# 100 instead of 96 tokens through gathered expert rows, with other transfers, another softmax placing and four gather buffers

## Chip, core and metric

One core of a Trainium2 chip. The metric is device time in microseconds (us) from launch to end; the median of three runs is given. Engines are named as in the profile: PE (matrix engine), DVE (vector), ACT (scalar), POOL (general), SP (queue that issues most loads). Everything is float32 unless noted.

## What is computed

One decoder layer for 256 tokens of width 2048. After attention and a first layer norm, x goes through a retrieval layer ("PEER"), and then through a gated embedding and a third norm. The retrieval layer is what the change is about:

```python
q = (xt @ wq).reshape(t, PEER_HEADS, PEER_QDIM)
...
va, ia = lax.top_k(sa, PEER_TOPK)
vb, ib = lax.top_k(sb, PEER_TOPK)
cand = (va[..., :, None] + vb[..., None, :]).reshape(t, PEER_HEADS, PEER_TOPK * PEER_TOPK)
cidx = (ia[..., :, None] * PEER_NKEYS + ib[..., None, :]).reshape(t, PEER_HEADS, PEER_TOPK * PEER_TOPK)
top, sel = lax.top_k(cand, PEER_TOPK)
eidx = jnp.take_along_axis(cidx, sel, axis=-1)
gates = jax.nn.softmax(top, axis=-1)
...
    act = jax.nn.gelu(jnp.einsum('thed,td->the', u[eb], xb).astype(jnp.float32))
    return jnp.einsum('the,thed->td', (gb * act).astype(xb.dtype), v[eb])
```

With 8 heads and 16 choices a head, each token uses 128 of 16384 rows of u and of v, each row 2048 numbers (8 KB).

## The kernel before

**Two ways for the experts.** `GROUPS` (L42) names the tokens whose expert rows are fetched one by one: tokens 0 to 63 and 64 to 95, `NSP` = 96 in all. The other `NDT` = 160 tokens are done densely: all 16384 experts are multiplied on PE, and the gates of those not chosen are zero.

*Dense path.* `u_block` (L903) loads 128 experts (1 MB, through SP, five buffers `WF` in turn), multiplies them with the 160 tokens (16 matmuls of 128x128 by 160 columns, which the profile shows as 32 instructions at L206), and ACT writes their gelu to the tile A (L906). `gate_work` (L838) makes the gate matrix from one-hot products on PE (L867, L868; five tokens in a group, L882), and DVE multiplies A by it (L877). `v_block` (L967) then multiplies A with v, 512 KB and 16 matmul instructions (L956) in each of 256 blocks. Two v blocks share a load.

*Gathered path.* `sparse_work` (L770) is a generator whose steps are put between the blocks. A step issues a mark (a tiny load on SP, L812), a copy on POOL that waits for the mark (L813, it paces), and an indirect DMA on POOL (L815) that fetches 128 rows, 1 MB, into one of `NGB` = 3 buffers `gb`. For a group of n tokens 128/n partitions hold each token, so n gathers serve the group, once for u and once for v: 96 + 96. `use` (L792) consumes a gather `NGB` - 1 steps later: for u a product and sum with the token's own row in `xq` (L794), for v a scaled addition to `y` (L798, L800). `sparse_out` (L825) adds the partitions of a token with matmuls against a 0/1 matrix `sel` (L832) and ACT copies the result to `yT` (L835).

*Order of work.* `gathers(n)` (L762) adds n to an account and runs one step for each whole unit: `GQ` = 1.3 for each of the last 13 of 16 query products (L206 into `ps_q`), `GU` = 0.715 for each u block, `GV` = 0.3575 for each v block. The rest is run off after block 108 of the second half of the v blocks (L1030), and `sparse_out` comes after block 113 (L1033). The last `STAG` = 6 v blocks are held back and run bank by bank (L1042), with `res2` (L1005: transposes on PE, residual and statistics on DVE) between them; the first half of `res2` is done at L1035 inside the loop.

*Top-k and gates.* `topk_work` (L730) is another generator. For the first 128 tokens each head's chain (DVE, with a product on POOL, L684) ends in `head_slots` (L715), which computes the expert numbers (L718) and places them by DMA (`place`, L722) in the index tile `eig` from which the gathers read. Then comes `gates(0)` (L697): subtract the maximum on DVE (L700), Exp on ACT (L702), sum, reciprocal and product on DVE; then the chain for tokens 128 to 255 (`topk_heads(1, ...)`), one step for each u block.

The order inside an engine's queue is made by a planner before the launch; it may move an instruction ahead of others, but those wrapped in `keep` stay in program order among themselves. An engine works its queue strictly in order, PE's weight loads aside. ACT's gelu at L906 is not kept, the Exp at L702 is.

## Time and profile before

| | us |
|---|---|
| median of three runs | 1829.22 |
| lowest, highest | 1827.53, 1829.93 |
| the profiled execution | 1826.57 |
| its span, first to last instruction | 1824.6 |
| PE busy in the span | 1786.7 |

The span starts at the first instruction; positions below are microseconds from there. The retrieval layer lies between 415 and 1708: queries 415 to 534, u blocks 534 to 1116, v blocks 1119 to 1703. The gate products run from 858 to 1265. A row of the view by stretches gives, for each engine, its busy time and in brackets its instructions, then the clock granted to PE (1.00 is full), the busy share of the 16 DMA engines, and GB/s. A row of the view by groups reads: line, engine, operation, output<-inputs, shape, count | busy us, mean ns of one | idle time before them and what ended it.

### The profile page before, as it was taken

Reading aid. Unit: us, or ns where it says so; the run is one execution under the profiler, and the core shown is the slowest. Engines: PE = TensorE matmul, PEld = TensorE weight load, DVE = VectorE, ACT = ScalarE, POOL = GpSimd, SP = SyncE. Lnnn points to the kernel's source line nnn. Section 1 sums busy time; section 2 is a strip of 40 time slices with the busy share of each in tenths; the row PEclk is TensorE's granted clock in tenths of the full one; section 3 lists DMA queues with packets and bytes.
Section 4 is the critical chain, followed back from the end, with each engine's and each line's share of the span. In section 5 each row is a group of like instructions: output and inputs, shape, how many; then the busy total and the mean of one; then the engine's idle time right before and its main releaser. Section 6 shows DMA issues by size and latency. Waiting matters only on the chain.

```text
span 1824.6 us, 30303 instructions
## 1 busy us (share of the span) xinstructions
PE 1786.7 (98%) x12094; PEld 1679.9 (92%) x12094; DVE 1045.2 (57%) x1643; ACT 544.4 (30%) x1365; POOL 500.6 (27%) x579
## 2 busy tenths in 40 slices
PE   8999999999999999999999999999999999999896
PEld 6888888888899999999999999999999999999766
DVE  5555588654677894543554544975433333343686
ACT  5677477642010001002333331862000000001532
POOL 0133033006445242322222212222234233220241
PEclk9999999999999999999999999999999999999998
DMA  7554644668789999999999999999999999996561
GB/s 278 187 171 163 231 145 156 231 212 266 306 316 374 420 420 416 395 420 401 415 379 383 380 391 353 420 419 350 421 421 420 415 416 415 419 421 267 212 258 53
DMA packets 98717, 599.33 MB, mean 328 GB/s; under 512 B 13072, under 2 KB 14912, under 8 KB 35600
## 3 DMA queue, kind: packets, MB, share of 16 engines
q1 hardware_dynamic: 66768, 384.24, 54.4%
q0 software_dynamic: 30080, 208.57, 28.5%
q10 hardware_dynamic: 1728, 4.59, 0.7%
q8 instruction: 95, 1.56, 0.3%
q14 instruction: 46, 0.38, 0.1%
HBM read 590.96 MB, written 6.29 MB: 327 GB/s over the span
## 4 chain that ended last, share of the span: by engine, by line
PE 82%; issue 6%; DVE 5%; DMA 4%; POOL 2%; ACT 1%; SPq 0%; DVEq 0%; POOLq 0%; ACTq 0%
PE ps_v L956 30%; PE ps_u L206 23%; PE ps_qk L195 7%; PE ps_qk L197 3%; PE ps_q L206 2%; PE ps_v L214 2%; PE ps_v L215 2%; PE ps_v L213 2%; PE ps_mix L213 1%; PE ps_mix L214 1%; PE ps_mix L215 1%; DMA wf<-peer_u 1%; PE ps_gate L214 1%; PE ps_gate L213 1%; PE ps_gate L215 1%
## 5 line engine op out<-in xcount | busy, mean ns | idle before, releaser
L206 PE MATMUL ps_u<-XF,wf 128*128 128x160 f32 x4096 | 572.4, 301 | 6.8 <-ACT A L906 6.6
L956 PE MATMUL ps_v<-A,wf 128*128 128x160 f32 x4096 | 569.1, 301 | 0.6 <-DVE A L877 0.6
L206 PEld LDWEIGHTS ps_u<-XF,wf 128*128 128x128 f32 x4096 | 560.3, 191 | 9.7 <-ACT A L906 8.8
L956 PEld LDWEIGHTS ps_v<-A,wf 128*128 128x128 f32 x4096 | 558.5, 191 | 1.6 <-DVE A L877 0.7
L800 DVE SCALAR_TENSOR_TENSOR y<-gb,ew,y 128x2048 f32<-128x2048 f32 x94 | 220.9, 2350 | 242.0 <-DMA gb<-v_rows,eig 241.8
L108 DVE TENSOR_TENSOR wl<-wf,wh 128x1024 fp32r<-128x1024 f32 (+1 forms) x201 | 222.7, 1132 | 98.3 <-ACT wh L107 97.0
L794 DVE SCALAR_TENSOR_TENSOR gb<-gb,xq 128x2048 f32<-128x2048 f32 x96 | 218.7, 2286 | 93.3 <-DMA gb<-u_rows,eig 90.5
L107 ACT CAST wh<-wf 128x1024 fp32r<-128x1024 f32 (+1 forms) x201 | 172.8, 889 | 111.7 <-PE ps_qk L195 29.4
L815 POOL DMA_INDIRECT gb<-u_rows,eig x96 | 101.3, 1055 | 334.4 <-DVE gb L794 213.9
L195 PE MATMUL ps_qk<-X,wh 128*128 128x512 f32 x512 | 185.2, 401 | 0.0
L815 POOL DMA_INDIRECT gb<-v_rows,eig x96 | 115.8, 1206 | 196.8 <-DVE y L800 148.8
L906 ACT ACTIVATE A<-ps_u 128x160 f32<-128x160 f32 x128 | 38.5, 303 | 434.7 <-PE ps_u L206 389.4
L813 POOL COPY pace<-mark 1x1 f32<-1x1 f32 x192 | 95.3, 496 | 252.1 <-DMA mark<-c_iota 251.4
L197 PE MATMUL ps_qk<-X,wl 128*128 128x256 f32 x512 | 146.1, 285 | 0.0
L859 ACT ACTIVATE hi<-eq,ghf 128x64 f16<-128x64 f16 x320 | 107.3, 335 | 52.5 <-DVE eq L853 48.5
L195 PEld LDWEIGHTS ps_qk<-X,wh 128*128 128x128 f32 x512 | 96.6, 189 | 21.9 <-issue 1.0
L206 PE MATMUL ps_q<-XF,wf 128*128 128x256 f32 x512 | 113.5, 380 | 0.0
L853 DVE TENSOR_TENSOR eq<-io,iaT 128x320 f16<-128x320 f16 x64 | 31.2, 488 | 133.8 <-ACT lo L860 133.8
L206 PEld LDWEIGHTS ps_q<-XF,wf 128*128 128x128 f32 x512 | 96.2, 191 | 12.0
L860 ACT ACTIVATE lo<-eq,glf 128x64 f16<-128x64 f16 x320 | 107.0, 334 | 0.0
L197 PEld LDWEIGHTS ps_qk<-X,wl 128*128 128x128 f32 x512 | 96.4, 188 | 2.5 <-issue 1.3
L835 ACT COPY XF<-ps_y 128x512 f32<-128x512 f32 x3 | 1.8, 585 | 253.2 <-PE ps_y L832 253.2
(232 smaller groups left out, 1791.2 us busy)
## 6 DMA issues: line engine op xcount, KB each, us to landing
wf<-peer_u SPq DMA_DIRECT2D x128, 1024.0 KB
wf<-peer_v SPq DMA_DIRECT2D x128, 1024.0 KB
wf<-w_qk SPq DMA_DIRECT2D x64, 512.0 KB
wf<-w_out SPq DMA_DIRECT2D x32, 512.0 KB
wf<-peer_wq SPq DMA_DIRECT2D x16, 1024.0 KB
wf<-ple_gate SPq DMA_DIRECT2D x16, 1024.0 KB
wf<-w_v SPq DMA_DIRECT2D x31, 512.0 KB
mark<-c_iota SPq DMA_DIRECT2D x192, 0.0 KB
```

The lines of the kernel that those rows point to most:

```text
L107: self.order(nc.scalar.copy(wh, src))
L108: self.order(nc.vector.tensor_tensor(wl, src, wh.bitcast(F32), op=ALU.subtract))
L195: nc.tensor.matmul(ps, wh[:, j * P:(j + 1) * P], xt[:, dt, :], start=dt == 0, stop=False)
L197: nc.tensor.matmul(ps[:, :T], wl[:, j * P:(j + 1) * P], xt[:, dt, :T], start=False, stop=dt == ND - 1)
L206: nc.tensor.matmul(ps[:, :T - t0], wf[:, dt * P:(dt + 1) * P], xt[:, dt, t0:], start=dt == 0, stop=dt == ND - 1)
L794: keep(nc.vector.scalar_tensor_tensor(g, g, 1.0, xq[i], op0=ALU.mult, op1=ALU.mult, accum_out=eact[i][:, j:j + 1]))
L800: keep(nc.vector.scalar_tensor_tensor(ys[i], g, ew[i][:, j:j + 1], ys[i], op0=ALU.mult, op1=ALU.add))
L813: keep(nc.gpsimd.tensor_copy(pace, mark))
L815: keep(nc.gpsimd.indirect_dma_start(out=g, out_offset=None, in_=a[kind], in_offset=bass.IndirectOffsetOnAxis(ap=eig[i][:, 0, j:j + 1], axi ...
L859: nc.scalar.mul(hi[:, j, :], eq[:, j, :], ghf[:, t])
L860: nc.scalar.mul(lo[:, j, :], eq[:, j, :], glf[:, t])
L956: return nc.tensor.matmul(ps[:, (j % 2) * NDT:(j % 2 + 1) * NDT], vf[:, j * P:(j + 1) * P], W_of(ia), start=False, stop=ia == NIA - 1 and ...
```

## The change

1. A third group of 4 tokens: 100 gathered tokens, 200 gathers, 156 dense tokens. Its rows share buffers with the first group (`tag=f"xq{i % 2}"`), are loaded when the second group's gather number 8 is issued, and its sum `y` lies in the gather buffer itself.
2. Four gather buffers; paces 1.8, 0.7 and 0.35.
3. A token's 128/n partitions are neighbours (before: n apart). So the expert numbers, the gates and the rows of a group each go by one DMA; for the rows the source is read 128/n times by a broadcast. A DVE copy into the new tile `es` orders the numbers of a whole group first. `sel` follows.
4. `gates(0)` runs beside the top-k of the other tokens: the subtraction after its fourth step, the Exp two steps later, the sum six steps after that. The gathered path multiplies no gate in before `gated` is set.
5. The rest of the gathers is run off after v block 119 (before: 108), `sparse_out` comes after block 121 (before: 113), and all of `res2` lies between the held blocks, whose matmuls are now kept in order. The two early loads of gate weights move from after blocks 116 and 119 to after 113 and 117.

```diff
-GROUPS = ((0, 64), (64, 32))
+GROUPS = ((0, 64), (64, 32), (96, 4))
-NGB = 3
-GQ = 1.3
-GU = 0.715
-GV = 0.3575
+NGB = 4
+GQ = 1.8
+GU = 0.7
+GV = 0.35
...
+    es = tkl.tile([P, 2, PH * TOPK], U32, name="es")
...
+        yield
+        yield
         keep(nc.scalar.activation(g, g, AF.Exp))
-        yield
+        for _ in range(6):
+            yield
         keep(nc.vector.tensor_reduce(gs[:, t], g, axis=AX.X, op=ALU.add))
...
-                place(i, slice(0, PH), 1)
+                slots(i, 1, by_slot(i, 1))
+            gated.append(t)
...
+    def slots(i, w, src):
+        t0, n = GROUPS[i]
+        nc.gpsimd.dma_start(eig[i][:, w],
+                            src[t0:t0 + n].rearrange("t (r j) -> t r j", j=n))
+    def by_slot(i, w):
+        t0, n = GROUPS[i]
+        src = eg[t0:t0 + n, w].bitcast(F32)
+        if n < PH:
+            return eg[:, w].rearrange("t h k -> t (h k)")
+        dst = es[t0:t0 + n, w].bitcast(F32)
+        nc.vector.tensor_copy(dst.rearrange("t (r h c) -> t h r c", h=PH, r=P // n),
+                              src.rearrange("t h (r c) -> t h r c", r=P // n))
+        return es[:, w]
     def head_slots(h):
...
-        place(0, slice(h, h + 1), 0)
-    def place(i, hs, w):
-        t0, n = GROUPS[i]
+        t0, n = GROUPS[0]
         m = n // PH
-        dst = eig[i].rearrange("p w (h m) -> p w h m", h=PH)
-        for q in range(P // n):
-            nc.gpsimd.dma_start(dst[q * n:(q + 1) * n, w, hs],
-                                eg[t0:t0 + n, w, hs, q * m:(q + 1) * m])
+        nc.gpsimd.dma_start(eig[0][:, 0, h * m:(h + 1) * m],
+                            eg[t0:t0 + n, 0, h].rearrange("t (r c) -> t r c", c=m))
...
-            place(i, slice(0, PH), 0)
-        yield from gates(0)
-        yield from topk_heads(1, 0, PH)
+            slots(i, 0, by_slot(i, 0))
+        second, first = topk_heads(1, 0, PH), gates(0)
+        for step in range(24):
+            next(second)
+            if step > 2:
+                next(first, None)
+            yield
+        yield from second
...
+        def tokens(i):
+            t0, n = GROUPS[i]
+            xq.append(gin.tile([P, D], F32, name=f"xq{i}", tag=f"xq{i % 2}"))
+            nc.gpsimd.dma_start(xq[i], a["s_x1"][t0:t0 + n, None, :].to_broadcast([n, P // n, D]))
+        tokens(0)
+        tokens(1)
...
-            if acts:
+            if acts and gated:
...
-                ys[i] = gin.tile([P, D], F32, name=f"y{i}", tag=f"xq{i}")
+                if i < 2:
+                    ys[i] = gin.tile([P, D], F32, name=f"y{i}", tag=f"xq{i}")
+                else:
+                    ys[i] = g
...
+                    if kind == "u_rows" and (i, j) == (1, 2 * NGB):
+                        tokens(2)
...
-        if ia == NIA - STAG - 14:
+        if ia in (NIA - STAG - 9, NIA - STAG - 5):
+            sg2.order = keep
+            parts0 += list(sg2.parts(a["ple_gate"][0, len(parts0) // 4]))
+        if ia == NIA - STAG - 3:
             while not run(sparse, 1):
                 pass
-        if ia == NIA - STAG - 9:
-            sparse_out()
-        if ia in (NIA - STAG - 8, NIA - STAG - 7):
-            for t in range(NT):
-                res2(t, 4 * (ia - NIA + STAG + 8), 4)
-        if ia in (NIA - STAG - 6, NIA - STAG - 3):
-            sg2.order = keep
-            parts0 += list(sg2.parts(a["ple_gate"][0, len(parts0) // 4]))
     held = [v_load(1, ia) for ia in range(NIA - STAG, NIA)]
-    for b in range(4):
-        for ia in range(NIA - STAG, NIA):
-            for j in (2 * b, 2 * b + 1):
-                v_mm(psv2[b], j, ia, held[ia - NIA + STAG])
-        v_out(1, b, psv2[b])
-        if b < 3:
-            for t in range(NT):
-                res2(t, 8 + 2 * b, 2)
+    sparse_out()
+    between = [(), ((0, 4),), (), ((4, 4), (8, 2)), (), ((10, 2),), (), ((12, 2),)]
+    for j in range(8):
+        for d0, nd in between[j]:
+            for t in range(NT):
+                res2(t, d0, nd)
+        for ia in range(NIA - STAG, NIA):
+            keep(v_mm(psv2[j // 2], j, ia, held[ia - NIA + STAG]))
+        if j % 2:
+            v_out(1, j // 2, psv2[j // 2])
```

More of the change, by code (lines that the diff above doesn't have):

```diff
@@ L655, in build @@
     keep = tc.keep_in_program_order
+    gated = []
     def topk_heads(t, h0, n):
@@ L719, in head_slots @@
                                        ibN[:NSP, 0, c], op0=ALU.mult, op1=ALU.add)
-        place(0, slice(h, h + 1), 0)
-    def place(i, hs, w):
-        t0, n = GROUPS[i]
+        t0, n = GROUPS[0]
         m = n // PH
-        dst = eig[i].rearrange("p w (h m) -> p w h m", h=PH)
-        for q in range(P // n):
-            nc.gpsimd.dma_start(dst[q * n:(q + 1) * n, w, hs],
-                                eg[t0:t0 + n, w, hs, q * m:(q + 1) * m])
+        nc.gpsimd.dma_start(
+            eig[0][:, 0, h * m:(h + 1) * m],
+            eg[t0:t0 + n, 0, h].rearrange("t (r c) -> t r c", c=m))
     def topk_work():
@@ L772, in sparse_work @@
         xq = []
-        for i, (t0, n) in enumerate(GROUPS):
-            xq.append(gin.tile([P, D], F32, name=f"xq{i}", tag=f"xq{i}"))
-            for q in range(P // n):
-                nc.gpsimd.dma_start(xq[i][q * n:(q + 1) * n, :], a["s_x1"][t0:t0 + n, :])
+        def tokens(i):
[4 more added lines that the diff above has]
+        tokens(1)
         made = []
@@ L1191, in _constants @@
         "c_ident": np.eye(P, dtype=np.float32),
-        **{f"c_sel{i}": (np.arange(P)[:, None] % n == np.arange(n)[None, :]).astype(np.float32)
+        **{f"c_sel{i}": (np.arange(P)[:, None] // (P // n) == np.arange(n)[None, :]).astype(np.float32)
            for i, (_, n) in enumerate(GROUPS)},
```

6 lines of the change are left out of this document (3 added, 3 removed).

## The prediction

> **What bounds the kernel now.** I read the page's first part and its groups first, then the view by stretches, then the DMA view of two stretches.
>
> ```profile
> PE 1786.7 (98%) x12094; PEld 1679.9 (92%) x12094; DVE 1045.2 (57%) x1643; ACT 544.4 (30%) x1365; POOL 500.6 (27%) x579
> ...
> L206 PE MATMUL ps_u<-XF,wf 128*128 128x160 f32 x4096 | 572.4, 301 | 6.8 <-ACT A L906 6.6
> L956 PE MATMUL ps_v<-A,wf 128*128 128x160 f32 x4096 | 569.1, 301 | 0.6 <-DVE A L877 0.6
> ```
>
> PE is busy for 98% of the span, and two groups of 4096 dense matmuls with 160 columns are 1141 us of it. What makes these shorter shortens the kernel, as long as their loads come in time. That second half is read from the stretches.
>
> ```profile
> core 0: us, PE busy (x) PEld busy (x) DVE busy (x) ACT busy (x) POOL busy (x), PEclk, DMA share, GB/s
> ...
> 415.00:534.00 119.00, 119.00 (x590) 105.96 (x589) 74.40 (x243) 15.28 (x39) 63.59 (x73) 1.00 0.80 285
> 534.00:560.00 26.00, 26.00 (x194) 26.00 (x193) 19.85 (x67) 4.01 (x7) 11.45 (x14) 1.00 0.94 367
> 560.00:570.00 10.00, 6.86 (x38) 6.62 (x38) 5.97 (x11) 2.48 (x6) 6.59 (x12) 0.83 0.99 377
> 570.00:635.00 65.00, 65.00 (x481) 65.00 (x480) 53.24 (x163) 4.64 (x16) 19.31 (x32) 1.00 1.01 405
> 635.00:670.00 35.00, 32.67 (x233) 31.40 (x232) 34.00 (x86) 2.52 (x9) 7.17 (x12) 1.00 1.01 420
> 670.00:860.00 190.00, 188.67 (x1391) 187.63 (x1390) 90.96 (x109) 19.34 (x62) 59.82 (x77) 1.00 1.00 411
> 860.00:1116.00 256.00, 256.00 (x2091) 254.06 (x2090) 127.79 (x160) 91.06 (x371) 54.40 (x77) 1.00 0.97 386
> 1116.00:1276.00 160.00, 159.22 (x1375) 155.19 (x1374) 115.52 (x127) 79.09 (x321) 42.41 (x56) 1.00 0.96 389
> 1276.00:1650.00 374.00, 374.00 (x2755) 374.00 (x2755) 144.74 (x62) 1.70 (x4) 110.75 (x119) 1.00 1.01 419
> ```
>
> The last two columns matter. In the query stage the DMA engines move 285 GB/s. From 570 on they are full (share 1.01) at 405 to 420, again from 1276 on at 419. Between, where the gate products slow PE down, 386 to 389 suffice. So two stretches have PE and DMA at their limits together.
>
> ```profile
> DMA packets 18716, 132.56 MB, mean 407 GB/s; under 512 B 2531, under 2 KB 2563, under 8 KB 2563
> ...
> q1 hardware_dynamic: 10467, 75.50, 56.6%
> q0 software_dynamic: 8224, 56.70, 42.7%
> ```
> ```profile
> DMA packets 21589, 156.53 MB, mean 419 GB/s; under 512 B 2504, under 2 KB 2504, under 8 KB 2504
> ...
> q1 hardware_dynamic: 12334, 89.04, 57.5%
> q0 software_dynamic: 8940, 65.00, 41.9%
> q10 hardware_dynamic: 288, 2.10, 1.4%
> ```
> ```profile
> q1 hardware_dynamic: 1472, 10.62, 51.0%
> q0 software_dynamic: 1421, 10.36, 50.0%
> ```
>
> These are the stretches 534:860, 1276:1650 and 590:640: q1 carries the weights, q0 the gathers, in MB. In 590:640 both queues have work all the time, and each gets half, 10.4 to 10.6 MB in 50 us, some 210 GB/s. A weight load of 1 MB (1.0486 million bytes) then takes 4.98 us. PE needs one each 4.35 us (32 instructions). So **gathers that are late take weights away from PE**:
>
> ```profile
> 561.81 0.31 ACT L702 ACTIVATE gate<-gate 128x128 f32<-128x128 f32 x1 [16.81 <-DVE gate L700]
> ```
> ```profile
> 563.79 6.42 PE L206 MATMUL ps_u<-XF,wf 128*128 128x160 f32 x33 [3.14 <-ACT A L906]
> ```
> ```profile
> 640.04 4.58 PE L206 MATMUL ps_u<-XF,wf 128*128 128x160 f32 x32 [0.41 <-ACT A L906]
> 645.01 4.59 PE L206 MATMUL ps_u<-XF,wf 128*128 128x160 f32 x32 [0.39 <-ACT A L906]
> 649.99 4.59 PE L206 MATMUL ps_u<-XF,wf 128*128 128x160 f32 x32 [0.38 <-ACT A L906]
> ```
>
> From 640 blocks start 4.97 us apart, the time of a load at half the bandwidth; I read the named releaser, ACT, as wrong there, since its gelu follows each block at once. The stall at 560 is another thing: ACT sits 16.81 us at the Exp of the first softmax, because DVE is late with the subtraction, the gelus behind it wait, and PE runs out of banks for 3.14 us. The clock of 0.83 in 560:570 costs 1.7 us more.
>
> **The change part by part.**
>
> *Fewer columns.* Rows of the chain of waits give the price of a column:
>
> ```profile
> 443.73 6.91 PE ps_q L206 x32
> ...
> 1275.97 386.85 PE ps_v L956 x2848
> ...
> 1662.83 7.07 PE ps_y L832 x64
> ```
>
> 256 columns: 6.91/32 = 215.9 ns; 160 columns: 386.85/2848 = 135.8 ns. That is 0.834 ns a column. With 64 or 32 columns an instruction still takes 7.07/64 = 110.5 ns, a floor well below 156 columns (132.5). Four columns less are 3.34 ns, for 8192 instructions 27.3 us: by share of the instructions 7.7 in 534:860, 9.4 in 860:1276, 9.2 in 1276:1650 and 1.0 after. The gate products fall from 640 to 624, each of 194 ns but overlapped:
>
> ```profile
> L868 PE MATMUL ps_G<-lo,ohb 128*128 128x64 f16 x320 | 33.5, 194 | 0.1
> ```
>
> Sixteen less save between 0 and 3.1 us; 0.5 taken, since the stretch shows them 10 at a time inside PE's busy time.
>
> *The third group in sparse_out.* 16 matmuls, 32 instructions of 4 columns, at the floor: 32 x 110.5 ns = +3.5 us, all on PE (between 0.4 at 4 columns' price and 3.5).
>
> So **PE alone** would give -27.3 - 0.5 + 3.5 = -24.3 us. The rest is what the loads and waits make of it.
>
> *The u blocks up to 860.* How many gathers are late when they begin:
>
> ```profile
> 415.00:534.00 119.00, 24.91 (x22) 12.25 (x12) 1.00 0.80 285
> 534.00:860.00 326.00, 121.15 (x106) 60.23 (x55) 0.99 1.00 407
> ```
>
> These are the same stretches for the tile gb alone: POOL issued 12 gathers before 534, while the accounts say 16 (13 x 1.3), so 4 to 5 are late. Now 23 are due. What holds them is not bandwidth (285) but the chain head by head: POOL waits for DVE's product, places the numbers, issues as many gathers as buffers are free, and DVE waits for the first of them:
>
> ```profile
> L794 DVE SCALAR_TENSOR_TENSOR gb<-gb,xq 128x2048 f32<-128x2048 f32 x96 | 218.7, 2286 | 93.3 <-DMA gb<-u_rows,eig 90.5
> ```
>
> A fourth buffer lets one more go in each of seven rounds, and one placing DMA of two falls away; each also costs DVE 2.29 us, 16 us for seven, in a queue that is busy 74.4 of 119. Between 0 and 7 more get done; I take 4, 16 by 534, so 7 are late. By block 72 (860) the accounts fall from 51.5 to 50.4 gathers. Before, 54 were moved (56.70/1.0486), 2.5 of the late ones made good. Now 4.6 are to be made good to stand the same, and the row load for the third group adds one: 56, 58.7 MB. With 75.5 of weights and 0.4 of rest 134.6 MB. At 407 GB/s that is 331 us, at 419, the full rate, 321; I take 325. PE alone would need 326 - 7.7 = 318 with today's stalls and 305.5 without (72 blocks of 4.24 us). So **the DMA queue, not PE, ends this stretch: 325 instead of 326, -1 in place of -7.7**. The softmax stall lies inside: while PE waits, gathers catch up. Its Exp comes five blocks (21 us) later in the program; DVE's subtraction comes later as well (16 us of products, then three top-k steps and three gathers at 5 us), so I do not count on the 4.8 us. The bounds: 310 if nothing is made good, 342 if none of the seven gets done.
>
> *860 to 1276.* DMA at 386 to 389 leaves 8% of room, PE ends: -9.4 - 0.5 = -9.9. DVE, busy 243 of 416, has room for the added gathers' 2.3 us each; it would be late next only where it is full (34.0 of 35 in 635:670).
>
> *1276 to 1650.* The same 86 loads (89.04 MB), 60.3 gathers (63.2 MB), 2.1 and 0.4: 154.7 MB, at 419 GB/s 369.3 us; PE wants 364.8. So between -9.2 and -4.7; with a load or so drawn from the five buffers, -7.
>
> *The end.* Less columns -1.0, the third group +3.5. And the wait for the last sum:
>
> ```profile
> 1634.91 0.96 POOL L815 DMA_INDIRECT gb<-v_rows,eig  x1 [0.16 <-issue]
> ```
> ```profile
> 1650.45 2.35 DVE L800 SCALAR_TENSOR_TENSOR y<-gb,ew,y 128x2048 f32<-128x2048 f32 x1 [3.90 <-DMA gb<-v_rows,eig]
> ```
> ```profile
> 1662.66 7.23 PE L832 MATMUL ps_y<-sel,y 128*128 128x64 f32 x64
> ```
>
> DVE ended at 1652.8, PE came at 1662.7: 9.9 us of slack. The last gather was due after block 105, eight blocks before sparse_out; now it is due at 119, two before. Six blocks of 2.12 us are 12.7 us, so PE waits 2.9 us; from 0 to 7 (a fourth gather in flight lands up to 5 us later, or the buffer is free earlier). Taken: +3. Behind it on PE's queue the held matmuls and the transposes of res2, which have no other cover. DVE's and ACT's share of res2 moves between the held blocks at the same work: 0. Sum of the end: +5.5.
>
> *At nothing.* POOL issues some 16 DMAs less; DVE makes three ordering copies and SP issues eight marks more. None of it ends a stretch, since PE and the full DMA queues cover it; where it hurries or holds the head chain, it does so within the bounds of the late gathers.
>
> *A rule against it.* Loading the rows:
>
> ```profile
> xq<-s_x POOLq DMA_DIRECT2D x2, 512.0 KB, 10.0
> xq<-s_x POOLq DMA_DIRECT2D x4, 256.0 KB, 13.4
> ```
>
> Both were read from 64 or 32 rows. The third group's 1 MB has 4 rows as its source's outer dimension. If it ran on 4 of 16 engines, it would take 1.0486 MB/(419/4 GB/s) = 10 us alone and 20 us beside the weights, and the gathers behind it on those engines as long; weights at half rate for 20 us cost PE 20 x (1 - 4.24/4.98) = 3 us. The Trainium skill, DMA: Bandwidth & Descriptors, "Why a DMA increments its semaphore by 16 and not by 1", says that the number of engines is the largest up to 16 that divides the outer dimension of both sides, which would make it 4; it notes exceptions for this queue. No run here shows it. It is a rival below, not in the sum.
>
> **Sum.** -1 - 9.9 - 7 + 5.5 = -12.4 us. The profiled execution, 1826.6 (span 1824.6 and 2.0 around it), would become 1814.2; it stood 2.65 under the median of 1829.22, so the median becomes **1816.8**.
>
> **The rivals.**
>
> - *PE gets all of it* (0.18): the fourth buffer and the idle DMA of the query stage keep gathers in time, and the softmax stall goes: -24.3 - 4.8 = -29.1, 1800. For it: 285 GB/s before 534. Against it: the head chain, not the bandwidth, holds gathers.
> - *The seven stay late* (0.10): 11 late at 534, 9 made good: 139 MB, 332 to 342 us, +11 in place of -1: -0.4, 1829, no change.
> - *Four engines for one load* (0.05): +3, 1820.
> - *Slower: ACT stands at the Exp* (0.12). Price: ACT stood 16.8 us and PE 3.1, so the banks cover 13.7. In the u blocks PE may stall 19.5 us (325 - 305.5) before this ends the stretch rather than DMA. It is slower by more than 3.7 us when PE stalls 36, of which 1.7 is clock, so ACT waits 48: the subtraction at about 607 if ACT comes at 559, after block 6. My estimate is 592 (561.5 + 16 + 15), a stall of some 21 that DMA asks for anyway. With 55 us of waiting: +11, 1840. For it: DVE was 97% busy in 635:670. Against: the planner may put gelus ahead of the Exp.
>
> **How the numbers follow.** My forecast, 1808 to 1825, has 0.55. Differences under 0.2% (3.7 us) can hardly be told from none. Faster: forecast, first and third rival, 0.78; same: nearly all of the second, 0.09; slower: 0.13. The range reaches to the first rival and to the seven late ones with the full price in both full stretches, 1799 to 1832.
>
> **What would show it.** Right: blocks 4.24 us apart where the gate products or an idle DMA leave room; 325 us from the first u block to the 73rd; 4.98 us apart while both queues hold half; weights stretch from the 33rd v load at 419 GB/s or more; PE idle before L832 with DVE L800 as releaser. Wrong: instructions of 156 columns at 135.8 ns; no blocks at 4.98 us; a wait of ACT at L702 over 40 us.

## The result, and the profile after

| us | before | after |
|---|---|---|
| median of four runs each | 1828.38 | **1840.53** |
| lowest, highest | 1826.13, 1829.93 | 1838.36, 1842.56 |
| the profiled execution | 1826.57 | 1840.73 |
| its span | 1824.6 | 1838.9 |

The change makes the kernel slower: the ratio after to before is 1.0067, with a 95% interval of 1.005 to 1.0085. The prediction was 1816.8, 24 us lower, and the time lies outside its range.

In the page of the changed kernel, the first part and the two large groups:

```profile
PE 1775.4 (97%) x12110; PEld 1663.2 (90%) x12110; DVE 1059.0 (58%) x1659; ACT 540.0 (29%) x1351; POOL 558.4 (30%) x580
...
L206 PE MATMUL ps_u<-XF,wf 128*128 128x156 f32 x4096 | 561.9, 299 | 24.1 <-DMA wf<-peer_u 23.0
L992 PE MATMUL ps_v<-A,wf 128*128 128x156 f32 x4096 | 553.5, 297 | 6.3 <-DMA wf<-peer_v 6.3
```

PE is busy 11.3 us less (before 1786.7) and the span is 14.3 us longer: what the columns gave went into waiting. Before, 6.8 us of idle time stood at the u blocks, and ACT was named for 6.6 of them. Now it is 24.1, with the weights' DMA named for 23.0, and 6.3 at the v blocks. Where this is shows in the view by stretches of the changed kernel:

```profile
core 0: us, PE busy (x) PEld busy (x) DVE busy (x) ACT busy (x) POOL busy (x), PEclk, DMA share, GB/s
415.00:534.00 119.00, 118.56 (x586) 104.83 (x585) 82.66 (x253) 18.06 (x43) 68.47 (x74) 1.00 0.85 331
534.00:815.00 281.00, 272.71 (x2024) 268.85 (x2023) 192.77 (x425) 26.36 (x78) 109.53 (x131) 1.00 1.01 415
815.00:850.00 35.00, 25.20 (x160) 23.05 (x158) 6.10 (x8) 11.11 (x46) 3.60 (x7) 0.90 1.03 255
850.00:890.00 40.00, 33.74 (x274) 33.13 (x274) 21.37 (x28) 11.19 (x46) 7.88 (x11) 0.96 0.98 382
890.00:1283.00 393.00, 390.69 (x3320) 386.59 (x3321) 225.80 (x265) 148.46 (x606) 121.20 (x119) 1.00 0.99 390
1283.00:1660.00 377.00, 375.60 (x2829) 374.66 (x2828) 140.07 (x60) 1.67 (x4) 116.74 (x122) 1.00 1.01 420
1660.00:1717.00 57.00, 52.08 (x372) 51.37 (x372) 27.35 (x38) 7.58 (x15) 5.96 (x6) 0.91 0.58 240
```

Two rows are out of line. From 815 to 850 the DMA engines are busy all the time (share 1.03) and move 255 GB/s, in a queue that moves 415 ahead of it. And in the last stretch PE's granted clock is 0.91 on average. The query stage moves more than before (331 for 285 GB/s).

For a sum over stages I use the starts of PE's blocks in the traces, counted from 0. In this table and the next, a "v block" is the pair that shares a load (32 instructions), so there are 128 of them, as of the u blocks:

| us | before | after | difference | predicted |
|---|---|---|---|---|
| u block 0 starts | 534.0 | 535.5 | +1.5 | 0 |
| u block 0 to u block 74 | 335.1 | 354.5 | **+19.4** | -1 |
| u block 74 to v block 32 | 406.8 | 393.3 | -13.5 | -9.9 |
| v block 32 to v block 120 | 382.5 | 375.6 | -6.9 | -7 |
| v block 120 to the last v matmul | 44.4 | 58.2 | **+13.8** | +5.5 |
| from there to the end | 121.9 | 121.8 | -0.1 | 0 |

Of the +19.4, a gain of 4.6 comes up to u block 62, and a loss of 24.1 between blocks 62 and 74: 78.0 us in place of 53.9. At 809.04, just ahead, POOL issues the third group's rows (L803, the load with 4 rows ahead). In the changed kernel's timeline of PE, with the idle time ahead of each row in brackets:

```profile
825.01 6.18 PE L206 MATMUL ps_u<-XF,wf 128*128 128x156 f32 x32 [0.35 <-DMA wf<-peer_u]
834.52 6.18 PE L206 MATMUL ps_u<-XF,wf 128*128 128x156 f32 x32 [3.33 <-DMA wf<-peer_u]
...
843.79 4.51 PE L206 MATMUL ps_u<-XF,wf 128*128 128x156 f32 x32 [2.82 <-DMA wf<-peer_u]
853.00 6.16 PE L206 MATMUL ps_u<-XF,wf 128*128 128x156 f32 x32 [4.71 <-DMA wf<-peer_u]
```

Blocks come 9.2 to 9.5 us apart and not 4.24, most of them wait for their weights, and the clock falls as well (6.18 us for 32 instructions in place of 4.5). Between blocks 62 and 74 the trace has 15.6 us of idle time of PE (0.4 before) and 10.2 us at half clock, which cost 5.1. The timeline of DVE shows the gathers standing behind the same load:

```profile
857.80 2.29 DVE L824 SCALAR_TENSOR_TENSOR gb<-gb,xq 128x2048 f32<-128x2048 f32 x1 [32.35 <-DMA gb<-u_rows,eig]
```

The DMA view of the changed kernel for 815 to 830 has the packets (q1 the weights, q0 the gathers and the row load):

```profile
DMA packets 956, 4.36 MB, mean 291 GB/s; under 512 B 424, under 2 KB 424, under 8 KB 424
...
q1 hardware_dynamic: 482, 3.47, 84.2%
q0 software_dynamic: 474, 0.89, 19.5%
```

q0 has 474 packets in 0.89 MB: most of them are not rows. 424 packets are under 512 bytes; in a stretch without this load about 100 are, as a row further down shows. In the trace they carry 4 bytes. In all, q0 has 464 of them between 800 and 840, beside 620 packets of 8 KB. Otherwise one comes with every eight 8 KB packets, which would be 78, so 386 are more than usual. 12 x 32 is 384: my reading is that 4 of the 16 engines carry 32 rows each, and the other 12 carry as many empty packets. The Trainium skill, DMA: Bandwidth & Descriptors, "Why a DMA increments its semaphore by 16 and not by 1", says that the engines are the largest number up to 16 that divides the outer dimensions of both sides; this count agrees with it. It names no price. The weights' queue moves 3.47 MB in these 15 us, 231 GB/s; in the next 20 us, from 830 to 850, it moves 2.29 MB, 115 GB/s.

The end, in the changed kernel's timeline and stretches of PE:

```profile
1664.86 8.75 PE L992 MATMUL ps_v<-A,wf 128*128 128x156 f32 x64 [1.57 <-DMA wf<-peer_v]
1676.50 4.51 PE L992 MATMUL ps_v<-A,wf 128*128 128x156 f32 x32 [2.90 <-DMA wf<-peer_v]
1681.46 4.51 PE L992 MATMUL ps_v<-A,wf 128*128 128x156 f32 x32 [0.46 <-DMA wf<-peer_v]
1685.81 7.45 PE L868 MATMUL ps_y<-sel,y 128*128 128x64 f32 x64
1693.08 6.97 PE L868 MATMUL ps_y<-sel,gb 128*128 128x4 f32 x32
1699.90 3.30 PE L992 MATMUL ps_v<-A,wf 128*128 128x156 f32 x12
```
```profile
1692.00:1693.00 1.00, 1.00 (x10) 0.83 0.51 213
1693.00:1702.00 9.00, 9.00 (x42) 0.50 0.06 24
1702.00:1703.00 1.00, 1.00 (x6) 0.55 0.00 0
```

PE does not wait for DVE ahead of the sum of the gathered rows, as I had predicted, but 5 us for the last v loads. And for 10 us the clock is 0.50: the 32 matmuls of 4 columns take 6.97 us, where 3.5 was their price, and the held blocks behind them start at half speed.

### The profile page after: what moved, and what is told of

It reads as the page before. It is cut to its first block, busy times and chain, and to the rows that moved or that the text cites. A ratio compares the mean times of both kernels' runs of the same rounds, so it can differ in the third digit from the quotient of the medians.

```text
span 1838.9 us, 30382 instructions
## 1 busy us (share of the span) xinstructions
PE 1775.4 (97%) x12110; PEld 1663.2 (90%) x12110; DVE 1059.0 (58%) x1659; ACT 540.0 (29%) x1351; POOL 558.4 (30%) x580
## 4 chain that ended last, share of the span: by engine, by line
PE 81%; DMA 15%; DVE 3%; ACT 1%; issue 0%; SPq 0%; DVEq 0%; POOL 0%; ACTq 0%; POOLq 0%
PE ps_v L992 26%; PE ps_u L206 21%; DMA wf<-peer_u 7%; PE ps_qk L195 7%; PE ps_q L206 6%; PE ps_qk L197 3%; DMA wf<-peer_v 3%; DMA gb<-u_rows,eig 2%; PE ps_v L214 2%; PE ps_v L215 2%; PE ps_v L213 2%; PE ps_mix L213 1%; PE ps_mix L215 1%; PE ps_mix L214 1%; PE ps_gate L214 1%; PE ps_gate L215 1%
## 5 line engine op out<-in xcount | busy, mean ns | idle before, releaser
L206 PE MATMUL ps_u<-XF,wf 128*128 128x156 f32 x4096 | 561.9, 299 | 24.1 <-DMA wf<-peer_u 23.0
L206 PEld LDWEIGHTS ps_u<-XF,wf 128*128 128x128 f32 x4096 | 550.0, 191 | 30.1 <-DMA wf<-peer_u 16.8
L992 PE MATMUL ps_v<-A,wf 128*128 128x156 f32 x4096 | 553.5, 297 | 6.3 <-DMA wf<-peer_v 6.3
L992 PEld LDWEIGHTS ps_v<-A,wf 128*128 128x128 f32 x4096 | 545.9, 190 | 8.5 <-DMA wf<-peer_v 8.0
L824 DVE SCALAR_TENSOR_TENSOR gb<-gb,xq 128x2048 f32<-128x2048 f32 x100 | 229.0, 2296 | 184.2 <-DMA gb<-u_rows,eig 184.1
L849 POOL COPY pace<-mark 1x1 f32<-1x1 f32 x200 | 111.7, 559 | 570.1 <-DMA mark<-c_iota 569.4
L942 ACT ACTIVATE A<-ps_u 128x156 f32<-128x156 f32 x128 | 38.3, 300 | 463.6 <-PE ps_u L206 364.7
L851 POOL DMA_INDIRECT gb<-u_rows,eig x100 | 127.0, 1270 | 140.5 <-DVE gb L824 79.2
L851 POOL DMA_INDIRECT gb<-v_rows,eig x100 | 136.3, 1363 | 53.6 <-issue 28.6
L214 PE MATMUL ps_gate<-wl,X 128*128 128x512 f32 (+1 forms) x144 | 53.8, 376 | 4.8 <-DVE wl L108 4.6
```

The costliest lines, as they stand in the source:

```text
L206: nc.tensor.matmul(ps[:, :T - t0], wf[:, dt * P:(dt + 1) * P], xt[:, dt, t0:], start=dt == 0, stop=dt == ND - 1)
L214: nc.tensor.matmul(ps, hi, wl, start=False, stop=False)
L824: keep(nc.vector.scalar_tensor_tensor(g, g, 1.0, xq[i], op0=ALU.mult, op1=ALU.mult, accum_out=eact[i][:, j:j + 1]))
L849: keep(nc.gpsimd.tensor_copy(pace, mark))
L851: keep(nc.gpsimd.indirect_dma_start(out=g, out_offset=None, in_=a[kind], in_offset=bass.IndirectOffsetOnAxis(ap=eig[i][:, 0, j:j + 1], axi ...
L992: return nc.tensor.matmul(ps[:, (j % 2) * NDT:(j % 2 + 1) * NDT], vf[:, j * P:(j + 1) * P], W_of(ia), start=False, stop=ia == NIA - 1 and ...
```

## The experiments

My theory after this: the shape of the third group's row load costs the 24 us, and the end's loss is the clock plus the waits. Rivals: any 1 MB at this place costs as much; the gain would be lost again later anyway; the clock falls because of the waits, not because of narrow matmuls. In all, 18 kernels ran. "Ratio" is that to the kernel before as measured beside each kernel (its median there was 1826.5 to 1827.7; the first row is the one of the result above); the four columns behind it are stage lengths of the profiled execution (u block 0 to 74, to v block 32, to v block 120, to the last v matmul).

| kernel | median us | ratio (95%) | u0-u74 | -v32 | -v120 | -last v |
|---|---|---|---|---|---|---|
| before | 1828.38 | 1 | 335.1 | 406.8 | 382.5 | 44.4 |
| the change | 1840.53 | 1.0067 (1.005-1.0085) | 354.5 | 393.3 | 375.6 | 58.2 |
| e1_rows4 | 1819.57 | 0.9965 (0.995-0.9979) | 337.0 | 389.7 | 376.1 | 58.8 |
| e1_indirect | 1813.24 | 0.9922 (0.9905-0.9938) | 332.2 | 389.7 | 374.9 | 58.9 |
| f1_pad32 | 1817.01 | 0.9956 (0.9943-0.9968) | 336.4 | 389.7 | 375.6 | 56.4 |
| f1_pad64 | 1811.63 | 0.9925 (0.9903-0.9948) | 335.9 | 389.7 | 376.4 | 50.9 |
| f2_ple | 1813.07 | 0.9933 (0.9911-0.9956) | 335.0 | 389.7 | 373.4 | 57.5 |
| g1_n96 | 1824.27 | 0.9997 (0.9985-1.0008) | 334.5 | 400.7 | 382.5 | 48.2 |
| h1_ngb3 | 1827.6 | 1.0005 (0.9996-1.0015) | 327.5 | 412.2 | 375.4 | 54.6 |
| h2_softmax | 1810.1 | 0.9911 (0.9894-0.9927) | 333.7 | 389.4 | 377.1 | 52.0 |
| h4_best | 1807.58 | 0.9902 (0.9885-0.9919) | 335.1 | 389.7 | 375.8 | 48.6 |
| i4_best2 | **1805.71** | 0.9879 (0.9863-0.9896) | 332.6 | 389.4 | 376.3 | 49.0 |

The kernels that add a load to the one before have a table of their own below.

### The shape of the row load

In `tokens`, e1_rows4:

```python
for k in range(n):
    m = P // n
    nc.gpsimd.dma_start(xq[i][k * m:(k + 1) * m, :],
                        a["s_x1"][t0 + k:t0 + k + 1, :].to_broadcast([m, D]))
```

> The changed kernel, with the third group's rows loaded by four DMAs, each of them one row repeated for 32 partitions, in place of one DMA whose source has 4 rows with 32 repeats; the bytes, the place and the queue are the same. Theory A (the shape with 4 rows ahead keeps few engines at work on it, and the loads behind it stand still): the stretch from the 62nd to the 74th u block, 78.0 us in the changed kernel and 53.9 in the one before, falls to about 54, DVE's wait of 32.4 us at the u dot goes, and the kernel takes about 1818 us, 20 to 24 less than the change. Rival B (1 MB more in a full queue at this place is the cost, whatever its shape): within 4 us of the change, 1837 to 1843. Rival C (the time gained there is lost again later, since the last gathers or the last stage end it): the stretch falls to 54 and the end by less than 10, 1830 to 1838.

and e1_indirect, with `tok` a new constant of 128 row numbers (96 + p // 32 for partition p):

```python
nc.gpsimd.indirect_dma_start(out=xq[i], out_offset=None, in_=a["s_x1"],
    in_offset=bass.IndirectOffsetOnAxis(ap=tok, axis=0))
```

> The changed kernel, with the third group's rows fetched by an indirect DMA whose 128 indices name the same 4 rows, each 32 times. Theory A (few engines because of 4 rows ahead): 128 descriptors spread over all engines, the stretch from the 62nd to the 74th u block at 54 to 57 us, the kernel at about 1818 us, as with four DMAs. Rival D (it is the same 4 rows of 8 KB, read 32 times each, that are slow to read, whichever engine asks): the stretch stays at 70 us or more, and the kernel within 6 us of 1840. Together with the run of four DMAs: if both are fast, it is the shape; if only this one is fast or only the other, it isn't the repeats alone.

The stretch from u block 62 to 74 falls from 78.0 to 58.9 and 56.3 us, and the kernel to 1819.6 and 1813.2. The same bytes at the same place, in another shape, are 21 and 27 us cheaper; 19.1 and 21.7 of them stand in this stretch. So the shape is the cause, as theory A says, and rivals B, C and D fall; whether it works by the number of engines is a question for the next section. The row 815 to 850 in the view by stretches, first of e1_rows4, then of e1_indirect:

```profile
815.00:850.00 35.00, 33.30 (x272) 31.65 (x271) 15.30 (x19) 14.10 (x58) 6.89 (x10) 1.00 1.02 370
```
```profile
815.00:850.00 35.00, 33.89 (x281) 32.65 (x280) 17.35 (x21) 14.68 (x61) 10.99 (x11) 1.00 1.01 423
```

255, 370 and 423 GB/s are the three shapes. DVE's longest wait for a gather falls from 32.4 to 10.3 and 7.4 us. Four DMAs with 32 repeats still cost some 10 us of slow packets (between 815 and 830), the indirect one nothing.

### The load by itself, in the kernel before

The other way round: the kernel before gets one load that nothing uses.

```python
if kind == "u_rows" and (i, j) == (0, 60):
    nc.gpsimd.dma_start(extra, a["s_x1"][96:100, None, :].to_broadcast([4, 32, D]))
```

> The kernel before, with one load added that nothing uses: the same 4 rows, each for 32 partitions, 1 MB, issued on the gathers' queue ahead of gather 60 of the u stage. Theory A: the u stage, which the DMA queue ends, loses 20 to 24 us there, and the kernel takes 1848 to 1853 us unless the v stages give some back. Rival B (any 1 MB costs its bytes, 1 MB at 421 GB/s = 2.5 us): 1829 to 1832. Rival E (only the changed gather schedule makes the load hurt, with 7 more gathers late): no more than 5 us.

> The kernel before, with 1 MB added at the same place as in the run with 4 rows, but from 128 rows for 128 partitions, unused. Theory A (the shape is the cost): its bytes alone, 2.5 to 3 us in the u stage, 1829 to 1832. Rival B (any 1 MB there costs the same): as much as the run with 4 rows.

1850.81 us (ratio 1.0139, 1.012 to 1.0158) and 1829.02 (1.0015, 1.0003 to 1.0027). The shape makes the difference again, but by luck the first figure fell into its range: without `keep` the loads went out at 443 us, and not where I had written. The loss of the 4 rows, 22.8 us, is a single stall between u blocks 4 and 8, and it is not a slow queue of weights: from 560 to 600 the DMA engines are busy for 0.65 of the time. POOL's queue, ACT's and PE's in the timelines of e3_dummy4:

```profile
483.50 1.06 POOL L818 DMA_INDIRECT gb<-u_rows,eig  x1 [34.17 <-DMA eig<-eg]
```
```profile
583.38 0.31 ACT L702 ACTIVATE gate<-gate 128x128 f32<-128x128 f32 x1 [38.29 <-DVE gate L700]
```
```profile
585.35 14.84 PE L206 MATMUL ps_u<-XF,wf 128*128 128x160 f32 x86 [24.61 <-ACT A L909]
```

The DMA of the first expert numbers was issued behind the load, POOL waited 34.17 us for it (17.43 in e3_dummy128), the top-k of the other heads waited for POOL, and the Exp came so late that ACT waited 38.29 us and PE 24.61. (This is the prediction's rival "ACT stands at the Exp", in another kernel; 38.29 less 24.61 is the 13.7 us that it said the banks cover.) So the load was repeated with `keep`, where it goes out at 809.5, and then with other shapes at the same place (804.8 to 812):

> The kernel before with the unused load of 4 rows for 128 partitions, 1 MB, this time kept in the program order of its queue, right ahead of gather 60 of the u stage (in the earlier run it went out at 443 us, ahead of the first gathers, and cost 20 us there). Theory A (the shape slows whatever is behind it in a full queue): PE waits for loads in the ten blocks after it and the u stage ends 18 to 24 us later, 1845 to 1852 us. Rival O (it hurts only where gathers are late, as in the query stage or in the changed kernel): under 8 us, 1829 to 1836.

> The kernel before with an unused load of 1 MB kept in order ahead of gather 60 of the u stage, as in the run with 4 rows that took 1844.5 us, but from 8 rows, each for 16 partitions. Theory R (the number of rows ahead is the number of engines that work on it): half the skew, 6 to 12 us, 1833 to 1839. Rival S (rows read many times are slow): nearly as with 4 rows, 1840 to 1846. Rival T (only fewer than 8 rows hurt): under 4 us, 1827 to 1831.

> The same load from 16 rows, each for 8 partitions. Theory R: all 16 engines work on it, no packets of 4 bytes beside it, its bytes alone, 2.5 us of a full queue: 1827 to 1831. Rival S: a third or more of the 18 us stays, 1833 or more.

> The same load from 128 rows for 128 partitions at the same place: the price of the place and the bytes without repeats. All theories: 2.5 to 4 us, 1828 to 1832; if it is more, the place itself costs, and the other runs are to be read against it.

> The kernel before with the unused 1 MB load kept ahead of gather 60 of the u stage, now with 16 repeats ahead of 8 rows in the source, so that rows follow one another and the whole set comes 16 times. Theory V (successive reads of one row by one engine are slow, and 16 ahead leave all engines at work): full bandwidth, as with 128 different rows, 1828 to 1832 us. Rival S (few rows read many times are slow in any order): 257 GB/s or less for 10 us, 1833 us or more.

> The same load from a single row repeated for 128 partitions, 128 ahead and so no engine left out. Both theories expect it slow: Theory V because each engine reads the one row 8 times in succession, rival S because there is one row; as with 16 rows or more, 1833 to 1840 us. Rival W (only the number of rows ahead matters, and the 16 ahead were too few for even work): as with 128 rows, 1828 to 1832.

| source of the 1 MB | run | median us | ratio (95%) | above before | u62-u74 |
|---|---|---|---|---|---|
| none | before | | 1 | | 53.9 |
| 4 rows, each 32 times | h3_dummy4k | 1844.53 | 1.0094 (1.0074-1.0113) | +17.7 | 71.4 |
| 8 rows, each 16 times | i1_dummy8 | 1837.81 | 1.0053 (1.0032-1.0074) | +10.2 | 65.0 |
| 16 rows, each 8 times | i2_dummy16 | 1833.4 | 1.0029 (1.0019-1.0039) | +5.8 | 60.9 |
| 16 repeats of 8 rows | j1_reps16 | 1833.6 | 1.0046 (1.0033-1.006) | +6.9 | 62.1 |
| 128 rows | i3_dummy128k | 1830.23 | 1.0014 (1.0002-1.0026) | +2.6 | 56.2 |
| 1 row, 128 times | j2_row1 | 1828.36 | 1.0013 (0.9999-1.0027) | +1.7 | 56.4 |

With 4 rows the kernel before slows down as well, a little less than expected (1844.5 for 1845 to 1852), and rival O falls: it costs far more than 8 us there. Theory R gets its sequence: 4, 8, 16 and 128 ahead cost 17.7, 10.2, 5.8 and 2.6. The DMA view of 815 to 830 shows the empty packets, in this order (4, 8, 16, 128 rows):

```profile
DMA packets 928, 4.34 MB, mean 289 GB/s; under 512 B 399, under 2 KB 399, under 8 KB 399
```
```profile
DMA packets 584, 3.42 MB, mean 228 GB/s; under 512 B 166, under 2 KB 166, under 8 KB 166
```
```profile
DMA packets 628, 4.60 MB, mean 306 GB/s; under 512 B 68, under 2 KB 68, under 8 KB 68
```
```profile
DMA packets 876, 6.33 MB, mean 422 GB/s; under 512 B 103, under 2 KB 103, under 8 KB 103
```

From 800 to 840, q0 has 381 more of them than usual with 4 rows, and 122 with 8 (8 engines x 16 would be 128). With 16 rows ahead no empty packets are left, and still this stretch moves 306 GB/s and not 422. The GB/s of these rows don't rank the price, the length of the slow time does: packets are slow for some 35 us with 4 rows, 20 with 8 and 10 with 16. So engines left out can't be the whole price. Theory R expected 1827 to 1831 for 16 rows and missed; i3 shows that the place and the bytes cost 2.6 us. The last two runs take away what I thought was left: one row read 128 times is as cheap as 128 rows, so reading a row again is not slow (rival S and theory V both fall), and j1, where other rows follow one another, is as slow as i2. Rival W's number came true, 1828 to 1832. What agrees with all of the runs is only this: with 128 ahead, packets keep their 0.31 us, and with 32, 16, 8 or 4 ahead those of both queues take 0.4 to 0.65 us on average for a while. Why they do, and why with 4 rows it goes on for 15 us after the empty packets have ended, stays open. The traces don't name the engine of a packet, so whether the shapes share the partitions out differently among the engines was not tested.

### The end of the v blocks

The third group's `sel` padded with zero columns, to 32 (f1_pad32), or the second's and third's to 64 (f1_pad64), both on e1_indirect:

```diff
-        sel.append(gin.tile([P, n], F32, name=f"sel{i}"))
+        sel.append(gin.tile([P, max(n, 64)], F32, name=f"sel{i}"))
...
-                    keep(nc.tensor.matmul(ps[:, j * n:(j + 1) * n],
+                    keep(nc.tensor.matmul(ps[:, j * m:(j + 1) * m],
```

> The changed kernel with the third group's rows fetched by an indirect DMA (the run that took 1813.2 us), and the third group's selection matrix padded with zero columns from 4 to 32, so that its 32 matmuls write 32 columns and the copy takes 4 of them. In the unpadded kernel the granted clock is 0.50 for 10 us from 1663.5, the narrow matmuls take 218 ns each and not 110. Theory F (the 4-column matmuls leave the array idle and pull the clock down): full clock, the last matmul of the gathered rows' sum 3.5 us earlier, the kernel at 1806 to 1809 us. Theory G (32 columns are already too few: the clock fell 2 us before the first 4-column matmul, after 2.5 us of 32-column ones): the clock falls as before, 1812 to 1815. Theory H (PE's waits of 1.5 to 2.0 us for loads some 10 us earlier pull it down): as G.

> As the run with 32 columns, but the second and the third group's selection matrices are both padded to 64 columns. A 64-column matmul took 113 ns in the first group at full clock, a 32-column one 110, so the padding itself costs at most 0.3 us. Theories F and G both: full clock throughout the sum of the gathered rows and the first held blocks, 5 to 7 us off the end, the kernel at 1806 to 1809 us. Theory H (the earlier waits pull the clock down): the 10 us at half clock stay, 1812 to 1815.

With 32 columns the clock falls as before, with 64 it stays, so theory G holds and F alone does not; rival H falls for this place, since PE waits for loads in both (3.1 and 2.4 us in the last stage). The timeline of PE in f1_pad32, then in f1_pad64:

```profile
1668.59 7.01 PE L876 MATMUL ps_y<-sel,gb 128*128 128x32 f32 x32
1675.41 3.31 PE L1000 MATMUL ps_v<-A,wf 128*128 128x156 f32 x12
```
```profile
1669.68 3.74 PE L876 MATMUL ps_y<-sel,gb 128*128 128x64 f32 x32
1673.26 1.81 PE L1000 MATMUL ps_v<-A,wf 128*128 128x156 f32 x12
```

7.01 and 3.74 us for the same 32 instructions, 3.31 and 1.81 for the 12 behind them. The last stage is 50.9 us in place of 58.9: 8 us. Not all of it is the clock: e1_indirect's trace has 13.7 us at half clock there, which cost 6.9, and 3.9 us of waits for loads in place of 2.4. f1_pad32, which differs from f1_pad64 in the padding alone, has 10.2 us at half clock, 5.1 of the 5.5 that its stage is longer. The median gained 1.6 only, 1811.6 for an expected 1806 to 1809, and f1_pad32 at 1817.0 fell outside either expectation: up to u block 74, where these kernels do not differ, the profiled executions scatter between 332.2 and 336.4 us, so for a few us I trust the stage and not the median.

The two early loads of the last stage's weights put back (f2_ple):

```diff
-        if ia in (NIA - STAG - 9, NIA - STAG - 5):
+        if ia in (NIA - STAG - 6, NIA - STAG - 3):
```

> The run with the indirect DMA (1813.2 us), with the two early loads of the last stage's weights put back three and two blocks later, where the kernel before has them. PE's waits for the last v blocks' loads are 4.7 us with them early. Theory I (these 2 MB at 424 GB/s, 4.9 us of a full queue, stand ahead of the v blocks' loads): the waits at v blocks fall to about 1, and the kernel to 1808 to 1811 us. Rival J (the queue is full with late gathers; whichever load comes first, the last one ends at the same time): PE's wait moves to the sum of the gathered rows or to the last stage, and the kernel stays within 2 us of 1813.

Rival J holds: 1813.07 us, and PE waits 4.4 us where it waited 4.7, only at later blocks. The queue is full at 418 to 426 GB/s until the last v load, and the order of what it carries does not matter. What does help is work for PE in these waits (h4_best, on f1_pad64):

```diff
+        if ia == NIA - STAG - 9:
+            sparse_out((0,))
...
-    sparse_out()
+    sparse_out((1, 2))
```

> The repaired kernel (1811.6 us) with the first group's 32 matmuls of the gathered rows' sum, 3.6 us, taken ahead of the last v blocks whose loads PE waits for 2.4 us. Theory P (the queue is full until then, and PE's work put into the waits is work taken off the end): the waits go and the last v matmul comes 2.4 us earlier, 1808 to 1810 us. Rival Q (the clock falls, or another wait takes the place): 1811 to 1814.

Theory P holds: PE's waits in the last stage fall from 2.4 to 0.5 us, the stage takes 48.6 in place of 50.9 us and the kernel 1807.6.

### The rest of the change

The changed kernel with two groups (g1_n96), and three parts undone on the repaired kernel (f1_pad64): the fourth buffer (`NGB = 3`, h1_ngb3), the softmax steps (h2_softmax), and the steps again on the best kernel (i4_best2). The last two put `gates(0)` in one piece ahead of the second top-k:

```diff
-        second, first = topk_heads(1, 0, PH), gates(0)
-        for step in range(24):
...
-        yield from second
+        yield from gates(0)
+        yield from topk_heads(1, 0, PH)
```

> The changed kernel without its third group: 96 tokens are gathered in groups of 64 and 32 as in the kernel before, all other parts of the change stay (fused transfers, a token's slots side by side, stepped softmax, four gather buffers, the rates, the order of the last stage), and the 4 tokens are computed with the other columns. By the prediction's terms for the columns the third group is worth 27.3 us less 3.5, and this kernel loses them: the column time of before, the Exp's stall of about 5 us gone. Expected, if the rest of the change is worth what the first u blocks gained in the changed kernel (5 us) and the last stage's waits go with fewer gathers: 1822 to 1826 us. If the fused transfers or the new order of the last stage cost time of their own: 1830 or more.

> The repaired kernel (indirect load of the third group's rows, selection padded to 64 columns; 1811.6 us) with three gather buffers as in the kernel before. The prediction gave the fourth buffer 4 more gathers by the first u block. Theory K (the buffer is what gets gathers done in the query stage): 3 to 4 gathers more are late, each 1.05 MB or 2.5 us of a full queue; u block 74 comes 7 to 10 us later and part of it stays, 1816 to 1822 us. Rival L (the fused transfers alone brought the gathers forward, or the queues even it out): within 2 us of 1811.6.

> The repaired kernel (1811.6 us) with the first softmax in one piece and ahead of the second top-k, as in the kernel before: its Exp stands on ACT while DVE is late with the subtraction. Theory M (the prediction's: while PE stands there the gathers catch up, so the DMA queue ends the u blocks at the same time): a stall of 3 to 5 us is seen about block 6, u block 74 within 1.5 us, 1810 to 1813 us. Rival N (the stall is paid in full): 1815 to 1818 us.

> The kernel with the indirect row load, 64-column selection and the first group's sum ahead of the last v blocks (1807.6 us), with the first softmax in one piece as before the change. Theory M (the stall at the Exp is paid for by the DMA queue's catching up, the steps are worth nothing): 1805 to 1809 us, u block 74 within 2 us of the stepped kernel. Rival N (the steps are worth the stall, now that less waits for DMA): 1810 to 1813.

**g1_n96** took 1824.27 us, as expected, and its ratio of 0.9997 can't be told from 1. Its last stage, 3.8 us longer than before, has no third group and no waits of PE for v loads, yet the clock falls in it, for 6.8 us, which cost 3.4. Its view by stretches:

```profile
1679.00:1680.00 1.00, 1.00 (x11) 0.89 0.00 0
1680.00:1686.00 6.00, 6.00 (x26) 0.50 0.00 0
1686.00:1687.00 1.00, 1.00 (x9) 0.70 0.00 0
```

So 32-column matmuls are enough. The kernel before has them too: its profiled execution kept its clock there, but five of its eight copies with an added load did not, during the narrow matmuls or right behind them: for 3.4 us in e3_dummy128, h3_dummy4k, i1_dummy8 and i2_dummy16, for 6.8 in i3_dummy128k, and the last stage is 1.7 and 3.3 us longer. Of the profiled executions with matmuls of 32 or fewer columns here, 11 of 15 lost the clock, of those with 64 none of five. What decides among the 15 is not shown; that it is where they fall in time is my reading.

**h1_ngb3** came out at 1827.6, above theory K's range, and K's mechanism is wrong. u block 74 comes 8.4 us sooner after block 0, not later, since fewer gathers share the queue (71 issued by then, and not 77). Nor did the buffer bring the gathers of the query stage: 16 are issued by u block 0 without it, 17 with it. The price stands at the first v block, in the timeline of PE:

```profile
1121.17 4.08 PE L1000 MATMUL ps_v<-A,wf 128*128 128x156 f32 x17 [7.16 <-DVE A L921]
```

POOL's waits for DVE's product, in the view of waits of h1_ngb3, then of f1_pad64:

```profile
POOL gb L858 <- DVE gb L831: 236.9, 47, 33.4
```
```profile
POOL gb L858 <- DVE gb L831: 52.0, 28, 6.5
```

With three buffers POOL waits 237 us for a free one. By u block 112, 93 gathers are issued where the accounts say 102; the v accumulations then stand in DVE's order among the last gate products, and PE waits for those: v block 0 comes 22.3 us after u block 127 starts and not 6.1. PE is idle for 8.3 us there, and the clock is halved for 13.7.

**h2_softmax** and **i4_best2** agree with theory M's time, not with its stall. In one piece the Exp costs nothing; ACT waits 5.5 us for the subtraction, fewer than the banks cover, and PE does not stop. From the timeline of ACT in i4_best2:

```profile
559.05 0.31 ACT L706 ACTIVATE gate<-gate 128x128 f32<-128x128 f32 x1 [5.50 <-DVE gate L704]
```

In the kernel before it waited 16.8 us there. Now DVE's subtraction ends 2.8 us earlier, and ACT comes to the Exp 8.5 us later, two gelus further on; which part of the change moved them was not tried. The steps are worth nothing: 1805.71 us without, the fastest kernel of this study, 1.2% below the kernel before.

## Why the prediction was wrong

- **The failed step is "A rule against it".** I had the mechanism, a load with 4 rows ahead on 4 of 16 engines, kept it out of the sum, gave it +3 us and a chance of 0.05. Its place was right: the row load is what costs, and the empty packets fit 4 engines and last 15 to 17 us, inside my 10 to 20. The size was wrong: I let weights run at half rate, 210 GB/s, for 20 us. In fact both queues together fell from 415 to 255 GB/s for 35 us, the weights to 115 for the last 20 of them, with 24.1 us for PE (e1_indirect takes 21.7 of them away again). The mechanism was right in part only: packets get slower with 16 rows ahead too, where no engine is left out, and of that I had nothing; its cause is open. My two rows for it, loads of 64 and 32 rows ahead, were no bound for 4 ahead, and I gave no upper end.
- **Fewer columns: right.** The chain of waits of the changed kernel has

```profile
1270.73 301.05 PE ps_v L992 x2272
```

  that is 132.5 ns an instruction, for a forecast of 132.5.
- **The u blocks up to 860, -1: right** once the load is repaired: -2.9 in e1_indirect, 0 in h4_best. From 629.77 to 649.65 blocks of the changed kernel start 4.97 us apart, as forecast for two queues that hold half each. The query stage moved 331 GB/s in place of 285, and 18 gathers were issued by u block 0 where I took 16 (17 in f1_pad64). The late ones were made good sooner than I thought: in f1_pad64 57 were issued by u block 48, as many as the accounts say. The fourth buffer I had right in direction and wrong in place: I gave it the 4 gathers more in the query stage, which come without it (16 in h1_ngb3, 12 before), and what it is worth stands at the first v block.
- **860 to 1276, -9.9: too little.** e1_indirect shows -17.1, and g1_n96 shows -6.1 without any change of columns. In the traces, PE goes over from a dense matmul to gate products 105 times in this stretch before the change, and 55 and 54 times in e1_indirect and g1_n96, and each time the first dense matmul behind them takes 83 ns longer (219 ns from start to start, the others 136, in g1_n96): 4.2 us for 51 changes fewer. The rest of the 6.1 is open. I had not looked at the order in which the planner mixes them.
- **1276 to 1650, -7: right** (-6.9; the row 1283 to 1660 has 420 GB/s).
- **The end, +5.5: failed by size and by cause.** +13.8 in the changed kernel. The +3 for a wait at the sum was wrong: PE waited 5 us at the v blocks' loads instead, in a queue that the late gathers kept full. The +3.5 for 32 narrow matmuls can't be read at full clock: with 4 columns every run has them at half clock for most of their time, and padded to 64 columns they took 3.74. The clock was not in my sum at all; 10.2 us at half clock cost 5.1. With the padding (f1_pad64) the end is +6.5.
- **The rivals.** Slower came about, but not by the Exp: ACT waited 5.4 us there, and that this rival's 1840 met the measured 1840.5 is chance. "Four engines" pointed at the right load with the wrong price. With the row load alone repaired, e1_indirect's span is 12.6 us shorter than before, close to the sum of -12.4; partly by chance, as the stretch from 860 to 1276 gained 7 more and the end lost 9 more.

## What to carry to other kernels

A load that repeats few rows over many partitions is to have all partitions ahead in its source: write it as an indirect load (or, where one row serves all, as that row 128 times), not as [4, 32, ...]. When a rule speaks against an edit and no row of the trace bounds its price, the upper end belongs in the range, and the edit is tried in another shape first. Count narrow matmuls by what they do to the clock behind them, not by their number alone; padding them to 64 columns cost 0.2 us for 32 of them (3.74 us, 3.5 at 110 ns each). And read in the trace where an added load went out before its time is explained.

## What the runs showed of the hardware

- A 1 MB load from 4 rows, each 32 times, slowed the 8 KB packets of both queues from 0.31 us to 0.4 to 0.65 on average for up to 35 us, and cost 17.7 to 24 us; from 8 rows 10.2, from 16 rows 5.8, from 128 rows or one row 1.7 to 2.6.
- 32 or 64 matmuls of 32 or fewer columns in a row, PE never idle in them, were met by half the granted clock for 3.4, 6.8, 10.2 or 13.7 us in 11 profiled executions of 15; 64 columns were not, in five of five (f1_pad64, h1_ngb3, h2_softmax, h4_best, i4_best2). The Trainium skill, TensorE: Matmul & The Clock Gate, "Part 1: The HAM clock gate", ties the half clock to idle windows of about 3.4 us; the lengths agree with one to four of them, but here PE was not idle, only narrow.
- The first dense float32 matmul behind a group of 16-bit gate products took 83 ns longer than others (219 ns from start to start for 136, in g1_n96).
